# Attention with the values stationary and the turned weights moving, in a two-layer hybrid block on one Trainium2 core

## Chip, core and metric

The kernel runs on one core of a Trainium2 chip. Time is device time in microseconds (us) of one execution. The engines are PE (TensorE; its weight loads are listed as PEld), DVE (VectorE), ACT (ScalarE), POOL (GpSimd) and SP (which issues the DMAs). Each engine works through its own instructions strictly in program order and waits for others through semaphores.

## The reference, cut to what matters

Two layers run one after the other over 256 tokens of width 1024. Each layer has a token mixer with three branches (MLA attention, mLSTM, dilated attention), gates and an output projection, and then a mixture of 16 experts. The change touches the two attentions of each layer. Both have 8 heads with values of width 64 and come down to this:

```python
s = jnp.einsum('bqhd,bkhd->bhqk', qi, k).astype(jnp.float32) * scale
s = jnp.where(kpos[None, :] <= qpos[:, None], s, -jnp.inf)
p = jax.nn.softmax(s, axis=-1)
return jnp.einsum('bhqk,bkhd->bqhd', p.astype(v.dtype), v)
```

The dilated attention joins three window patterns; since there are only 256 tokens, the kernel does all three as one masked softmax, with the count of patterns that reach a key as a logarithm in the mask. What follows both branches is a product of the attention's output with a 512 x 1024 weight.

## The kernel before

All big products ("dense", lines 474 to 476) keep full precision by splitting each operand into a high part and a rest: a weight chunk is loaded by DMA into a slot, ACT copies it rounded (high part) and DVE subtracts (rest), both on line 365, and three matmuls of 128x128 by 128x512 are summed for each block. One dense product of 256 tokens by 1024 by 512 is 48 such matmuls. Between its other work DVE also multiplies the modulation weights of this and the next layer (line 284, 1024 columns each, both operands in SBUF).

Everything outside a few pinned places is ordered by the framework's scheduler: the program's text gives a stream of instructions, and the scheduler lays them out for each engine in a fixed order, in which the dense matmuls of the next projections fill the places where an attention waits. That order is fixed before the run. There is no reordering when an operand comes late.

`softmax_pv` does one attention, once for MLA and once for dilated attention in each layer, so four times. It goes through two blocks of 128 queries: t=0 with 128 keys, t=1 with 256. For each block:

- PE makes the scores of 8 heads (line 794 in MLA, line 951 in dilated attention);
- DVE adds the mask and takes the row maximum (line 731) and scales it (lines 734 and 736);
- ACT takes the exponential with its row sum (line 739), into P;
- PE turns P, 128x128 at a time (line 745), 8 times for t=0 and 16 for t=1, and ACT copies the turned weights out of PSUM into T (line 746);
- PE multiplies: T is stationary and the 64 value columns of a head move (line 750), 8 or 16 matmuls in float32, which the profile shows as two instructions each;
- DVE inverts the row sums (line 751) and multiplies the output by them while it leaves PSUM (line 752).

Then `y_transposed` turns the output (tokens on partitions) into the operand of the branch's dense product: 8 transposes on PE (line 765), two copies on ACT (line 768) and two subtractions on DVE (line 769). The mLSTM branch uses the same function with a scale.

GpSimd (POOL) has little to do: rotary embedding in MLA (lines 662 to 671), a subtraction in the router (line 1089), memsets and a few DMAs.

Of the kernel before, what the change touches and what calls it, by code (L numbers as in the profile page):

```python
# [12 lines left out]
def _warn_once_fixed(msg, *args, **kwargs):  # L13
# [6 lines left out]
F32 = mybir.dt.float32  # L20
F32R = mybir.dt.float32r
I32 = mybir.dt.int32
AF = mybir.ActivationFunctionType
OP = mybir.AluOpType
# [14 lines left out]
C_ID, C_TRI, C_TRIS, C_MLA, C_DIL, C_MLM, C_COS, C_SIN, C_IOTA = (  # L39
    0, 128, 256, 384, 640, 896, 1024, 1088, 1152)  # L40
# [31 lines left out]
def tile_block(ctx: ExitStack, tc: tile.TileContext, x_in, c_in, cst_in, sv_in, aux_in, wada_in, ws_in, out, depth=L):  # L72
    nc = tc.nc
    PE, DVE, ACT, POOL, SP = nc.tensor, nc.vector, nc.scalar, nc.gpsimd, nc.sync
# [8 lines left out]
    def fs_tile(i, dtype=F32):  # L83
        return persist.tile([128, 2048], dtype, name=f"fs{i}")

    fs = Slots([fs_tile(i) for i in range(NB)], fs_tile)

    def xs_tile(i, dtype=F32R):
        return persist.tile([128, 2048], dtype, name=f"xs{i}")
# [4 lines left out]
    xs = Slots([xs_tile(i) for i in range(4)], xs_tile, F32R)  # L94
    rs = Slots([rs_tile(i) for i in range(NR)], rs_tile, F32R)

    def mmt(name="mm"):
        return psum.tile([128, 512], F32, name=name)

    cst = persist.tile([128, N_CST], F32, name="cst")  # L100
# [79 lines left out]
    def cut(h):  # L180
        return A0 if h < 2 else 512
# [81 lines left out]
    for hf in range(2):  # L263
        hs = slice(512 * hf, 512 * hf + 512)
        p = mmt("sm")
# [76 lines left out]
    def layer(l, tail):  # L342
# [185 lines left out]
        else:  # L528
# [21 lines left out]
            for n_, (k0, k1) in enumerate(groups):  # L550
# [11 lines left out]
                p = nxt_p  # L562
# [6 lines left out]
                for j, do in enumerate((first_chunk, second_chunk, third_chunk)):  # L569
# [3 lines left out]
                    n = cut(h_)  # L573
# [68 lines left out]
        for t in range(2):  # L642
            ts = slice(128 * t, 128 * t + 128)
# [10 lines left out]
        va = v_s[:, :1024].rearrange("p (t n) -> p t n", t=2)  # L654
# [18 lines left out]
        scq = work.tile([128, 2, 8], F32, name="scq", bufs=1)  # L673
        for t in range(2):
            ts = slice(128 * t, 128 * t + 128)
# [34 lines left out]
        fs.put(cq_s, up_s, up2_s)  # L710
        pump()

        def softmax_pv(kq, masks, scale, vv, out_s):

            for t in range(2):
                nk = 128 * (t + 1)
                per = 512 // nk
                P_s, T_s = fs.get(), fs.get()
                P = P_s[:, :8 * nk].rearrange("p (h n) -> p h n", h=8)
                T = T_s[:, :8 * nk].rearrange("p (b h n) -> p b h n", b=t + 1, h=8)  # L720
                den = work.tile([128, 8], F32, name="den")
                mx = work.tile([128, 8], F32, name="mx")
                for g in range(8 // per):
                    p = mmt("sm").rearrange("p (h n) -> p h n", h=per)
                    h0 = g % 2 + 4 * (g // 2)
                    hs = slice(h0, h0 + 2 * per - 1, 2)
                    for j in range(per):
                        kq(t, h0 + 2 * j, p[:, j])
                    for j in range(per):
                        h = h0 + 2 * j  # L730
                        DVE.tensor_tensor_reduce(p[:, j], p[:, j], masks[:, 128 * (1 - t):], 1.0, -3.0e38,
                                                 OP.add, OP.max, mx[:, h:h + 1])
                    if scale is None:
                        DVE.tensor_scalar(mx[:, hs], mx[:, hs], -1.0, None, op0=OP.mult)
                    else:
                        DVE.scalar_tensor_tensor(mx[:, hs], mx[:, hs], -1.0, scale[:, t, hs], op0=OP.mult, op1=OP.mult)
                    for j in range(per):
                        h = h0 + 2 * j
                        ACT.activation(P[:, h], p[:, j], AF.Exp, scale=1.0 if scale is None else scale[:, t, h:h + 1], bias=mx[:, h:h + 1],
                                       accum_out=den[:, h:h + 1])  # L740
                for b in range(t + 1):
                    for g in range(2):
                        p = mmt("sm").rearrange("p (h n) -> p h n", h=4)
                        for j in range(4):
                            PE.transpose(p[:, j], P[:, 4 * g + j, 128 * b:128 * b + 128], ident)
                        ACT.activation(T[:, b, 4 * g:4 * g + 4], p, AF.Copy)
                po = mmt("sm").rearrange("p (h d) -> p h d", h=8)
                for h in range(8):
                    for b in range(t + 1):
                        PE.matmul(po[:, h], T[:, b, h], vv[:, b, 64 * h:64 * h + 64], start=b == 0, stop=b == t)  # L750
                DVE.reciprocal(den, den)
                DVE.tensor_tensor(out_s[:, t].rearrange("p (h d) -> p h d", h=8), po,
                                  den[:, :, None].to_broadcast([128, 8, 64]), op=OP.mult)
                fs.put(P_s, T_s)

        def y_transposed(y, scale=None):

            yt_s = xs.get(F32R)
            yt = yt_s.rearrange("p (a b n) -> p a b n", a=2, b=4)
            for bb in range(2):  # L760
                p = mmt("sm").rearrange("p (b n) -> p b n", b=2)
                for b in range(2):
                    for t in range(2):
                        c = (2 * bb + b) * 128
                        PE.transpose(p[:, b, 128 * t:128 * t + 128], y[:, t, c:c + 128], ident)
                if scale is None:
                    s = slice(2 * bb, 2 * bb + 2)
                    ACT.activation(yt[:, 0, s], p, AF.Copy)
                    DVE.tensor_tensor(yt[:, 1, s], p, yt[:, 0, s].bitcast(F32), op=OP.subtract)
                else:  # L770
                    for b in range(2):
                        s = 2 * bb + b
                        ACT.activation(yt[:, 0, s], p[:, b], AF.Copy, scale=scale(s))
                        DVE.scalar_tensor_tensor(yt[:, 1, s], p[:, b], scale(s), yt[:, 0, s].bitcast(F32),
                                                 op0=OP.mult, op1=OP.subtract)
            return yt_s, yt

        qT_s, kT_s = fs.get(), fs.get()
# [2 lines left out]
        for t in range(2):  # L781
            ts = slice(128 * t, 128 * t + 128)
            for src, dst, g in ((qc, qT, V_GQ), (kc, kT, V_GK)):
                for gg in range(2):
                    p = mmt("sm")[:96].rearrange("p (h n) -> p h n", h=4)
# [2 lines left out]
                    o = dst[:, 4 * gg:4 * gg + 4, ts]  # L788
                    ACT.activation(o, p, AF.Copy, scale=sv[:96, g:g + 1])
        fs.put(qc_s, kc_s)  # L790
        ya_s = fs.get()
        ya = ya_s[:, :1024].rearrange("p (t n) -> p t n", t=2)
        def kq_a(t, h, p):
            PE.matmul(p, qT[:, h, 128 * t:128 * t + 128], kT[:, h, :128 * (t + 1)], start=True, stop=True)

        softmax_pv(kq_a, cst[:, C_MLA:C_MLA + 256], scq, va, ya)
        fs.put(qT_s, kT_s, v_s)
        yaT_s, yaT = y_transposed(ya)
        fs.put(ya_s)
        pump()  # L800


# [105 lines left out]
        hg = work.tile([128, 4], F32, name="hg", bufs=1)  # L908
        DVE.tensor_scalar(hg, col(V_HG, 4), 0.5, None, op0=OP.mult)
        ybT_s, ybT = y_transposed(yb, lambda s: hg[:, s:s + 1])  # L910
        fs.put(mo_s)
        pump()


        dn_s, dT_s, dv_s = fs.get(), fs.get(), fs.get()
        dn = dn_s.rearrange("p (a t n) -> p a t n", a=2, t=2)
        dT = dT_s.rearrange("p (a b n) -> p a b n", a=2, b=4)
        dv = dv_s[:, :1024].rearrange("p (t n) -> p t n", t=2)
        yc = dv_s[:, 1024:].rearrange("p (t n) -> p t n", t=2)
        dq8 = work.tile([128, 1], F32, name="dq8", bufs=1)  # L920
        POOL.tensor_scalar(dq8, col(V_DQ), 0.125, None, op0=OP.mult)
        for a in range(2):
# [13 lines left out]
            for bb in range(2):  # L936
                p = mmt("sm").rearrange("p (b n) -> p b n", b=2)
# [11 lines left out]
        def kq_c(t, h, p):  # L949
            r0 = 64 * (h % 2)  # L950
            PE.matmul(p, dT[r0:r0 + 64, 0, h // 2, 128 * t:128 * t + 128], dT[r0:r0 + 64, 1, h // 2, :128 * (t + 1)],
                      start=True, stop=True)

        softmax_pv(kq_c, cst[:, C_DIL:C_DIL + 256], None, dv, yc)
        fs.put(dT_s)
        ycT_s, ycT = y_transposed(yc)
        fs.put(dv_s)
        pump()


# [2 lines left out]
        for b, (yT_s, yT) in enumerate(((yaT_s, yaT), (ybT_s, ybT), (ycT_s, ycT))):  # L963
# [10 lines left out]
            g = g_s.rearrange("p (t n) -> p t n", t=2)  # L974
# [4 lines left out]
            if b == 1:  # L979
# [6 lines left out]
                p = mmt("sm")[:, :160]  # L986
# [3 lines left out]
            for hf in range(2):  # L990
                ps = dense(yT[:, 0], yT[:, 1], 4)
                hs = slice(512 * hf, 512 * hf + 512)
# [15 lines left out]
        for kk, p in transposed(mg):  # L1008
            s = slice(2 * kk, 2 * kk + 2)
# [16 lines left out]
        def small(name, *shape):  # L1026
            return work.tile([128] + list(shape), F32, name=name, bufs=1)
# [217 lines left out]
        ex, d = small("ex", 2, 4), small("d", 2, 4)  # L1245
# [102 lines left out]
    for l in range(depth):  # L1348
        tail = layer(l, tail)
# [130 lines left out]
```

## Time and profile before

| | us |
|---|---|
| median of 3 runs (817.21 to 821.32) | 818.74 |
| the profiled execution | 815.11 |
| its span, first to last instruction | 813.3 |
| PE busy | 772.1 (95%) |
| DVE busy | 568.4 (70%) |
| ACT busy | 385.7 (47%) |
| POOL busy | 32.9 (4%) |

Busy is the share of the span in which the engine had an instruction running. Matmuls are pipelined and their ends are modelled, so how fast PE really goes is read from the distance between the starts of its instructions. Layer 0 takes the first half of the span; its MLA attention lies at 80 to 106 us and its dilated attention at 143 to 166 us. Layer 1 has them at 464 to 490 us and 541 to 565 us.

### The profile page before, as it was taken

The page shows a single profiled execution, that of the slowest core. Times are in us where ns is not written, and L with a number is a line of the kernel's source. Part 1 is how long each engine was busy: PE and PEld are TensorE (multiplying, and loading weights), DVE is VectorE, ACT ScalarE, POOL GpSimd, SP SyncE. Part 2 cuts the span into 40 slices and gives each one's busy share as a digit, 9 for nine tenths or more (in the row PEclk, how much of TensorE's full clock was granted, in tenths as well). Part 3 has the DMA queues.
Part 4 walks back from the last instruction along what each step waited for, and adds up shares of the span by engine and source line. Part 5 has one row for each costly group of instructions (what it writes and reads, how often), then busy time and mean ns, then how long its engine had stood idle before and what let it go on. Part 6 is the DMA issues. An engine that isn't in the chain of part 4 may idle for free. (4 is left out here: it accounts for less than half of the span.)

```text
span 813.3 us, 11024 instructions
## 1 busy us (share of the span) xinstructions
PE 772.1 (95%) x3772; PEld 535.4 (66%) x3772; DVE 568.4 (70%) x1422; ACT 385.7 (47%) x851; POOL 32.9 (4%) x62
## 2 busy tenths in 40 slices
PE   4999999999999979999969999999999997999996
PEld 2886888788887753333358687888888876543333
DVE  6889989978899575232488988998647576633224
ACT  5477757754355451111277674676454552411111
POOL 0103000000000000000000300000000001000000
PEclk9999999999999989999989998999999998999999
DMA  8984654889999558999847367568986636499991
GB/s 338 408 329 155 246 221 163 320 299 373 361 370 365 208 235 365 420 421 420 349 147 251 112 262 255 207 253 310 343 304 226 215 110 245 185 423 422 421 413 58
DMA packets 36109, 234.37 MB, mean 288 GB/s; under 512 B 4017, under 2 KB 4689, under 8 KB 10450
## 3 DMA queue, kind: packets, MB, share of 16 engines
q1 hardware_dynamic: 35410, 231.52, 73.5%
q0 software_dynamic: 576, 2.10, 0.7%
q8 instruction: 31, 0.51, 0.2%
q14 instruction: 28, 0.23, 0.1%
q10 hardware_dynamic: 64, 0.02, 0.0%
HBM read 232.55 MB, written 1.06 MB: 287 GB/s over the span
## 5 line engine op out<-in xcount | busy, mean ns | idle before, releaser
L365 ACT ACTIVATE rs<-wa 128x512 fp32r<-128x512 f32 (+1 forms) x224 | 135.3, 633 | 87.9 <-PE mm L475 63.3
L474 PE MATMUL mm<-rs,rs 128*128 128x512 f32 (+1 forms) x432 | 171.9, 401 | 5.0 <-ACT rs L565 4.3
L365 DVE TENSOR_TENSOR rs<-wa,rs 128x512 fp32r<-128x512 f32 (+1 forms) x224 | 148.5, 683 | 38.2 <-ACT rs L365 25.4
L475 PE MATMUL mm<-rs,rs 128*128 128x512 f32 (+1 forms) x432 | 174.3, 404 | 0.4 <-DVE rs L462 0.3
L476 PE MATMUL mm<-rs,rs 128*128 128x512 f32 (+1 forms) x432 | 173.9, 403 | 0.0
L284 DVE SCALAR_TENSOR_TENSOR wa<-wa,cb 128x1024 f32<-128x1024 f32 x90 | 108.0, 1215 | 0.1
L474 PEld LDWEIGHTS mm<-rs,rs 128*128 128x128 f32 x432 | 81.9, 191 | 21.5 <-ACT rs L565 5.5
L475 PEld LDWEIGHTS mm<-rs,rs 128*128 128x128 f32 x432 | 82.9, 192 | 16.7 <-DVE rs L566 1.1
L476 PEld LDWEIGHTS mm<-rs,rs 128*128 128x128 f32 x432 | 83.0, 192 | 15.8 <-issue 1.1
L1207 PE MATMUL mm<-wa,xs 128*64 128x512 f32 x168 | 64.4, 595 | 0.0
L1215 DVE SCALAR_TENSOR_TENSOR th<-th,mm 128x256 f32<-128x256 f32 x16 | 6.7, 421 | 81.3 <-ACT th L1214 81.3
L1207 PE MATMUL mm<-fs,xs 128*64 128x512 f32 x184 | 60.8, 595 | 0.0
L109 ACT ACTIVATE fs<-fs 128x512 fp32r<-128x512 f32 x32 | 20.2, 630 | 68.2 <-DVE fs L1238 68.2
L1214 ACT ACTIVATE th<-mm 128x256 f32<-128x256 f32 x16 | 6.1, 384 | 97.4 <-PE mm L1207 97.4
L1238 DVE TENSOR_TENSOR fs<-mm,fs 128x512 f32<-128x512 f32 x32 | 22.0, 688 | 32.8 <-PE mm L1236 32.8
L1207 PE MATMUL mm<-rs,xs 128*64 128x512 f32 x160 | 42.8, 595 | 0.0
L474 PE MATMUL mm<-rs,xs 128*128 128x512 f32 x96 | 37.6, 392 | 0.0
L476 PE MATMUL mm<-rs,xs 128*128 128x512 f32 x96 | 37.5, 391 | 0.0
L1236 PE MATMUL mm<-wa,hid 128*64 128x512 f32 x80 | 36.5, 599 | 1.1 <-ACT hid L1224 1.1
L475 PE MATMUL mm<-rs,xs 128*128 128x512 f32 x96 | 37.4, 390 | 0.0
L1207 PEld LDWEIGHTS mm<-wa,xs 128*64 128x64 f32 x168 | 19.1, 137 | 26.9 <-issue 26.6
L1236 PE MATMUL mm<-fs,hid 128*64 128x512 f32 x96 | 36.5, 598 | 0.0
(334 smaller groups left out, 1313.2 us busy)
## 6 DMA issues: line engine op xcount, KB each, us to landing
wa<-in_ws_dram SPq DMA_DIRECT2D x85, 1024.0 KB, 7.0
fs<-in_ws_dram SPq DMA_DIRECT2D x45, 1024.0 KB, 14.8
wa<-in_wada_dram SPq DMA_DIRECT2D x40, 1024.0 KB, 5.4
rs<-in_ws_dram SPq DMA_DIRECT2D x30, 1024.0 KB, 13.3
wa<-in_wada_dram SPq DMA_DIRECT2D x10, 512.0 KB, 10.0
wa<-in_ws_dram SPq DMA_DIRECT2D x6, 512.0 KB, 9.0
fs<-in_wada_dram SPq DMA_DIRECT2D x6, 512.0 KB, 10.0
fs<-row POOLq DMA_DIRECT2D x4, 512.0 KB, 7.3
```

Of the source, the lines that this page charges most:

```text
L109: return ACT.activation(h, src, AF.Copy), DVE.tensor_tensor(l, src, h.bitcast(F32), op=OP.subtract)
L284: DVE.scalar_tensor_tensor(w, w, 0.5, cb, op0=OP.mult, op1=OP.mult, accum_out=mods[l][:, 2 * i + j:2 * i + j + 1])
L365: pinned(ACT.activation(h[:, cs_], r[:, cs_], AF.Copy), DVE.tensor_tensor(lo[:, cs_], r[:, cs_], h[:, cs_].bitcast(F32), op=OP.subtract))
L474: PE.matmul(o, ah[:, kb + k, ts], hv[:, k], start=st, stop=False)
L475: PE.matmul(o, al[:, kb + k, ts], hv[:, k], start=False, stop=False)
L476: PE.matmul(o, ah[:, kb + k, ts], lv[:, k], start=False, stop=en)
L1207: queued(PE.matmul(pgu[64 * i:64 * i + 64], a, wv[i][:, k], start=kb == 0, stop=kb == 7))
L1214: ACT.activation(th, pgu[:, :256], AF.Tanh, scale=0.5)
L1215: DVE.scalar_tensor_tensor(th, th, 1.0, pgu[:, :256], op0=OP.add, op1=OP.mult)
L1236: queued(PE.matmul(py[hf][i_], hid_[:, f, i_], wv[i][:, f, hs], start=f == 0, stop=f == 1))
L1238: DVE.tensor_tensor(y, py[hf], rows[:, 1, hs], op=OP.mult)
```

## The change

The output of an attention is now made turned. The values of a head (128 keys by 64) are the stationary operand and the turned weights (128 keys by 128 queries) move; the result is 64 value columns by 128 queries. Head 2hh writes PSUM partitions 0 to 63 and head 2hh+1 partitions 64 to 127 of the same columns. So the output is already the operand of the next product, and the 8 transposes, the copies and the subtractions of `y_transposed` are gone for these two branches; a copy on ACT and a subtraction on DVE for each block of queries (lines 760 and 761) make the high part and the rest straight from PSUM.

The row sums lie on query partitions, which the turned output no longer has. So the weights are divided before they are turned: DVE inverts the sums (line 743), and POOL multiplies P by them in two halves of four heads (line 746), with 512 columns each for t=0 and 1024 for t=1. The transposes (now line 750), the copies into T (line 751) and the products (line 758) come after that. `y_transposed` stays for mLSTM.

```diff
@@ -710,8 +710,10 @@
-        def softmax_pv(kq, masks, scale, vv, out_s):
+        def softmax_pv(kq, masks, scale, vv):
+
+            yt_s = xs.get(F32R)
+            yt = yt_s.rearrange("p (a b n) -> p a b n", a=2, b=4)
             for t in range(2):
                 nk = 128 * (t + 1)
...
@@ -738,22 +740,29 @@
                         ACT.activation(P[:, h], p[:, j], AF.Exp, scale=1.0 if scale is None else scale[:, t, h:h + 1], bias=mx[:, h:h + 1],
                                        accum_out=den[:, h:h + 1])
-                for b in range(t + 1):
-                    for g in range(2):
+                DVE.reciprocal(den, den)
+                for g in range(2):
+                    hs = slice(4 * g, 4 * g + 4)
+                    POOL.tensor_tensor(P[:, hs], P[:, hs], den[:, hs, None].to_broadcast([128, 4, nk]), op=OP.mult)
+                    for b in range(t + 1):
                         p = mmt("sm").rearrange("p (h n) -> p h n", h=4)
                         for j in range(4):
                             PE.transpose(p[:, j], P[:, 4 * g + j, 128 * b:128 * b + 128], ident)
-                        ACT.activation(T[:, b, 4 * g:4 * g + 4], p, AF.Copy)
-                po = mmt("sm").rearrange("p (h d) -> p h d", h=8)
-                for h in range(8):
+                        ACT.activation(T[:, b, hs], p, AF.Copy)
+
+                po = mmt("sm").rearrange("p (h n) -> p h n", h=4)
+                for hh in range(4):
                     for b in range(t + 1):
-                        PE.matmul(po[:, h], T[:, b, h], vv[:, b, 64 * h:64 * h + 64], start=b == 0, stop=b == t)
-                DVE.reciprocal(den, den)
-                DVE.tensor_tensor(out_s[:, t].rearrange("p (h d) -> p h d", h=8), po,
-                                  den[:, :, None].to_broadcast([128, 8, 64]), op=OP.mult)
+                        for i in range(2):
+                            h = 2 * hh + i
+                            PE.matmul(po[64 * i:64 * i + 64, hh], vv[:, b, 64 * h:64 * h + 64], T[:, b, h], start=b == 0, stop=b == t)
+                ts = slice(128 * t, 128 * t + 128)
+                ACT.activation(yt[:, 0, :, ts], po, AF.Copy)
+                DVE.tensor_tensor(yt[:, 1, :, ts], po, yt[:, 0, :, ts].bitcast(F32), op=OP.subtract)
                 fs.put(P_s, T_s)
-
-        def y_transposed(y, scale=None):
+            return yt_s, yt
+
+        def y_transposed(y, scale):
...
@@ -763,16 +772,11 @@
-                if scale is None:
-                    s = slice(2 * bb, 2 * bb + 2)
-                    ACT.activation(yt[:, 0, s], p, AF.Copy)
-                    DVE.tensor_tensor(yt[:, 1, s], p, yt[:, 0, s].bitcast(F32), op=OP.subtract)
...
-        softmax_pv(kq_a, cst[:, C_MLA:C_MLA + 256], scq, va, ya)
+        yaT_s, yaT = softmax_pv(kq_a, cst[:, C_MLA:C_MLA + 256], scq, va)
         fs.put(qT_s, kT_s, v_s)
-        yaT_s, yaT = y_transposed(ya)
-        fs.put(ya_s)
...
-        softmax_pv(kq_c, cst[:, C_DIL:C_DIL + 256], None, dv, yc)
-        fs.put(dT_s)
-        ycT_s, ycT = y_transposed(yc)
-        fs.put(dv_s)
+        ycT_s, ycT = softmax_pv(kq_c, cst[:, C_DIL:C_DIL + 256], None, dv)
+        fs.put(dT_s, dv_s)
```

The scheduler lays the engines' orders out anew. On PE, the first piece below is the second block of the dilated attention in layer 0, before. Lines 474 to 476 are dense matmuls of the gates, `fs_77` is P, `rs` are split weights; "x8" counts instructions of one kind in a row.

```order
L750 MATMUL sm<-fs_74,fs_71 128x64 x8
L951 MATMUL sm<-fs_76 128x256 x8
L476 MATMUL mm<-rs_87,rs_83 128x512
L474 MATMUL mm<-rs_87,rs_83 128x512
L475 MATMUL mm<-rs_87,rs_84 128x512
L476 MATMUL mm<-rs_87,rs_83 128x512
L745 MATMUL sm<-cst,fs_77 128x128
L474 MATMUL mm<-rs_87,rs_83 128x512
L475 MATMUL mm<-rs_87,rs_84 128x512
L476 MATMUL mm<-rs_87,rs_83 128x512
L745 MATMUL sm<-cst,fs_77 128x128 x2
```

The same place in the changed kernel; at "..." stand 22 more dense matmuls.

```order
L750 MATMUL sm<-cst,fs_74 128x128 x8
L475 MATMUL mm<-rs_86,rs_84 128x512
L476 MATMUL mm<-rs_86,rs_83 128x512
L758 MATMUL sm<-fs_75,fs_76 64x128 x8
L951 MATMUL sm<-fs_77 128x256 x8
L474 MATMUL mm<-rs_86,rs_83 128x512
L475 MATMUL mm<-rs_86,rs_84 128x512
L476 MATMUL mm<-rs_86,rs_83 128x512
...
L750 MATMUL sm<-cst,fs_73 128x128 x16
L758 MATMUL sm<-fs_72,fs_76 64x128 x16
```

The transposes stood in ones and twos among the dense matmuls, four dense matmuls after the scores. Now 25 dense matmuls stand between the scores and the transposes, and then 16 transposes and 16 products follow each other without a dense matmul among them. In the eight blocks of the kernel, in order, 34, 28, 33 and 25 dense matmuls (layer 0) and 35, 27, 33 and 25 (layer 1) stand between the scores and the first transpose.

On DVE, the same block before, from the last two mask steps on. Line 284 is a modulation multiply, line 365 the rest of a weight chunk.

```order
L734 TENSOR_SCALAR mx<-mx 128x2
L284 SCALAR_TENSOR_TENSOR wa_67,mod_122<-wa_67,cb 128x1024
L731 ISA sm,mx<-sm,cst 128x256
L731 ISA mx 128x1
L284 SCALAR_TENSOR_TENSOR wa_68,mod_122<-wa_68,cb 128x1024
L734 TENSOR_SCALAR mx<-mx 128x2
L365 TENSOR_TENSOR rs_87<-wa_66,rs_87 128x512
L284 SCALAR_TENSOR_TENSOR wa_68,mod_122<-wa_68,cb 128x1024
L751 RECIPROCAL den<-den 128x8
L365 TENSOR_TENSOR rs_87<-wa_66,rs_87 128x512
```

The same place in the changed kernel:

```order
L736 TENSOR_SCALAR mx<-mx 128x2
L284 SCALAR_TENSOR_TENSOR wa_67,mod_122<-wa_67,cb 128x1024
L736 TENSOR_SCALAR mx<-mx 128x2
L284 SCALAR_TENSOR_TENSOR wa_68,mod_122<-wa_68,cb 128x1024
L365 TENSOR_TENSOR rs_86<-wa_69,rs_86 128x512
L743 RECIPROCAL den<-den 128x8
L289 TENSOR_TENSOR mod_122<-mod_122,sv_91 128x8
L284 SCALAR_TENSOR_TENSOR wa_68,mod_122<-wa_68,cb 128x1024
L365 TENSOR_TENSOR rs_86<-wa_69,rs_86 128x512
```

The reciprocal has one modulation multiply fewer ahead of it (and two rests of weight chunks fewer, which stood among the first masks, above the piece). Behind it a modulation multiply comes up at once; and now POOL's two multiplies, all 16 transposes and the products wait for that reciprocal, where only the last output multiply did.

## Rows read from the trace of the kernel before

**Rows 1.** The page, busy time of each engine, share of the span and instructions.

```profile
PE 772.1 (95%) x3772; PEld 535.4 (66%) x3772; DVE 568.4 (70%) x1422; ACT 385.7 (47%) x851; POOL 32.9 (4%) x62
```

**Rows 2.** Windows: us, each engine's busy us (instructions), granted PE clock, DMA share, GB/s.

```profile
80.00:106.00 26.00, 26.00 (x168) 22.37 (x167) 22.61 (x73) 17.56 (x51) 0.00 (x0) 1.00 0.73 274
...
500.00:507.00 7.00, 7.00 (x21) 4.59 (x18) 4.69 (x12) 3.18 (x7) 0.00 (x0) 0.51 0.65 246
```

**Rows 3.** Timeline of PE in the gates: start us, us, engine, line, operation, shapes, count.

```profile
229.62 0.39 PE L475 MATMUL mm<-rs,rs 128*128 128x512 f32 x1
...
230.07 0.39 PE L474 MATMUL mm<-rs,rs 128*128 128x512 f32 x1
```

**Rows 4.** Timeline of PE in layer 0: attention products and output transposes (two stretches).

```profile
101.03 3.46 PE L750 MATMUL sm<-fs,fs 128*128 128x64 f32 x30
...
106.05 0.82 PE L765 MATMUL sm<-cst,fs 128*128 128x128 f32 x6
```

**Rows 5.** Timeline of PE in the experts, where two 64-column products share the array.

```profile
332.71 0.59 PE L1236 MATMUL mm<-wa,hid 128*64 128x512 f32 x1
332.72 0.59 PE L1236 MATMUL mm<-fs,hid 128*64 128x512 f32 x1
333.14 0.59 PE L1236 MATMUL mm<-wa,hid 128*64 128x512 f32 x1
...
335.29 0.59 PE L1236 MATMUL mm<-fs,hid 128*64 128x512 f32 x1
335.81 0.44 PE L1222 MATMUL mm<-cst,th 128*128 128x128 f32 x2
```

**Rows 6.** Timeline of layer 0, MLA: scores of t=0 (PE), reciprocals and output multiply (DVE).

```profile
81.05 1.95 PE L794 MATMUL sm<-fs,fs 96*128 96x128 f32 x16
82.76 0.47 PE L474 MATMUL mm<-rs,rs 128*128 128x512 f32 x1
...
89.75 0.19 DVE L751 RECIPROCAL den<-den 128x8 f32<-128x8 f32 x1
...
92.48 0.69 DVE L752 TENSOR_TENSOR fs<-sm,den 128x512 f32<-128x512 f32 x1 [0.83 <-PE sm L750]
...
99.29 0.20 DVE L751 RECIPROCAL den<-den 128x8 f32<-128x8 f32 x1
```

**Rows 7.** The same in layer 0, dilated attention, with idle time and its releaser.

```profile
143.53 1.52 PE L951 MATMUL sm<-fs 64*128 64x128 f32 x16
144.99 0.51 PE L476 MATMUL mm<-rs,rs 128*128 128x512 f32 x1
...
150.81 0.19 DVE L751 RECIPROCAL den<-den 128x8 f32<-128x8 f32 x1
...
152.88 2.10 PE L951 MATMUL sm<-fs 64*128 64x256 f32 x16
154.91 0.50 PE L476 MATMUL mm<-rs,rs 128*128 128x512 f32 x1
...
157.14 0.33 PE L745 MATMUL sm<-cst,fs 128*128 128x128 f32 x1 [1.04 <-ACT fs L739]
...
161.98 0.20 DVE L751 RECIPROCAL den<-den 128x8 f32<-128x8 f32 x1
```

**Rows 8.** POOL's multiplies by shape, and a stretch of POOL and DVE in layer 0.

```profile
L1089 POOL TENSOR_TENSOR fs<-xs,fs 128x512 fp32r<-128x512 f32 x4 | 5.0, 1260 | 49.0 <-ACT xs L1088 49.0
...
64.56 1.38 POOL L668 TENSOR_TENSOR fs<-fs,fs 128x256 f32<-128x256 f32 x1 [27.87 <-DVE rs L365]
65.90 0.72 POOL L669 TENSOR_TENSOR fs<-fs,fs 128x256 f32<-128x256 f32 x1
...
64.66 0.69 DVE L365 TENSOR_TENSOR rs<-wa,rs 128x512 fp32r<-128x512 f32 x1
...
66.18 0.47 DVE L701 TENSOR_SCALAR sh<-sh 128x8 f32<-128x8 f32 x1
...
69.24 0.16 DVE L701 TENSOR_SCALAR sh<-sh 128x8 f32<-128x8 f32 x1
```

**Rows 9.** DVE's modulation multiply, timeline of layer 0.

```profile
147.24 1.22 DVE L284 SCALAR_TENSOR_TENSOR wa<-wa,cb 128x1024 f32<-128x1024 f32 x1
```

More of the change, by code (lines that the diff above doesn't have):

```diff
@@ L765, in y_transposed @@
                         PE.transpose(p[:, b, 128 * t:128 * t + 128], y[:, t, c:c + 128], ident)
-                if scale is None:
-                    s = slice(2 * bb, 2 * bb + 2)
-                    ACT.activation(yt[:, 0, s], p, AF.Copy)
-                    DVE.tensor_tensor(yt[:, 1, s], p, yt[:, 0, s].bitcast(F32), op=OP.subtract)
[L770 to L775, printed above, removed]
+                for b in range(2):
+                    s = 2 * bb + b
+                    ACT.activation(yt[:, 0, s], p[:, b], AF.Copy, scale=scale(s))
+                    DVE.scalar_tensor_tensor(yt[:, 1, s], p[:, b], scale(s), yt[:, 0, s].bitcast(F32),
+                                             op0=OP.mult, op1=OP.subtract)
             return yt_s, yt
@@ L790, in layer @@
         fs.put(qc_s, kc_s)
-        ya_s = fs.get()
-        ya = ya_s[:, :1024].rearrange("p (t n) -> p t n", t=2)
         def kq_a(t, h, p):
             PE.matmul(p, qT[:, h, 128 * t:128 * t + 128], kT[:, h, :128 * (t + 1)], start=True, stop=True)
-        softmax_pv(kq_a, cst[:, C_MLA:C_MLA + 256], scq, va, ya)
+        yaT_s, yaT = softmax_pv(kq_a, cst[:, C_MLA:C_MLA + 256], scq, va)
         fs.put(qT_s, kT_s, v_s)
-        yaT_s, yaT = y_transposed(ya)
-        fs.put(ya_s)
         pump()
```

## Prediction

> **What bounds the kernel now.** I read the page's busy times first: PE is busy for 95% of the span, DVE for 70%, POOL for 4% [rows 1]. An average says little, so I went to the windows around the attentions. From 80 to 106 us, the MLA attention of layer 0, PE is busy in all 26.00 us and DVE in 22.61 [rows 2]. The timeline says whether a busy PE is also a fast one: in the gates, two dense matmuls after another start 0.45 us apart, so 0.226 us for 512 columns [rows 3], and around the attention the same spacing holds between the transposes. So in these stages an attention costs PE time only, because dense matmuls fill every wait. There is one exception: in the second block of the dilated attention PE stood idle for 1.04 us until the first exponential was there [rows 7]; I take the same for layer 1, so 2 us in all. A gain here must come from PE's own work, and any wait that the fixed order does not cover is lost in full.
>
> **What the change takes off PE.** The 8 transposes of line 765 go, four times: 32. Six of them take 0.82 us with the last one's tail [rows 4]; the products on line 750, with the same weight load, start (3.46 - 0.27)/29 = 0.11 us apart when the last one's tail is taken off [rows 4]. At 0.11 us, 32 transposes are 3.5 us. The products: 24 matmuls of two instructions for each attention, 192 in all, at 0.11 us: 21.1 us. They become 192 instructions with 128 moving columns, of which two at a time share the array. The trace of before has nothing quite like it. From below: the experts' products with 64 columns of weights start in pairs 0.01 us apart, a pair every 0.43 us for 512 columns [rows 5]; for a quarter of the columns that is 0.11 us a pair, 96 pairs, 10.6 us. From above: the dilated scores of 128 columns need 1.46 us for 16 instructions (143.53 to 144.99, [rows 7]), 0.09 each, 17.5 us; but their order puts only some of them in pairs. The new ones alternate between the two halves as the experts' do, so I take 10.6 us: a gain of 10.5 us (3.6 at the other end). Leaving the paired form costs something: the last pair to the next transpose is 0.52 us against 0.43 [rows 5]. Entering may cost as much, so 0.2 us for each of 8 bursts, 1.6 us. PE's work falls by 3.5 + 10.5 - 1.6 = 12.4 us.
>
> DVE loses eight output multiplies of 0.69 us (one in [rows 6]), 5.5 us; copies and subtractions stay as many. As DVE is not what ends last here, I count nothing for that.
>
> **What it puts on the path.** POOL's two multiplies now stand between the reciprocal and the transposes. A multiply of 512 columns takes 1.26 us on POOL and one of 256 takes 0.72 [rows 8], so each 256 more cost 0.54 and 1024 columns 2.34 us. A block needs two: 2.5 us for t=0, 4.7 us for t=1. No such broadcast of a sum stands in the rows; 256-column multiplies with a broadcast table (line 669) are the nearest. What covers it on PE are the scores and then 34, 28, 33 and 25 dense matmuls before the first transpose, and the first half's transposes. I count from the start of a block's scores; layer 1 is taken as layer 0.
>
> - MLA, t=0. The reciprocal ends at 89.94 - 81.05 = 8.9 us [rows 6], POOL at 11.4. PE: scores 1.7, 34 x 0.226 = 7.7, four transposes 0.44: it needs the second half at 9.85. Late by 1.6 us.
> - MLA, t=1. From the output multiply's start to the reciprocal's end are 7.0 us (92.48 to 99.49, [rows 6]); now a copy on ACT comes first, 0.7: 7.7, and POOL ends at 12.4. PE: scores twice 1.7, 28 x 0.226 = 6.3, eight transposes 0.9: 10.6. Late by 1.8.
> - Dilated, t=0. Reciprocal at 151.00 - 143.53 = 7.5 [rows 7], POOL at 10.0; PE 1.46 + 7.45 + 0.44 = 9.35. Late by 0.65.
> - Dilated, t=1. The reciprocal ended 9.3 us after the scores began (152.88 to 162.18, [rows 7]). In the new order one modulation multiply (1.22 by its row, [rows 9]; 1.15 to the next start) and two weight rests (0.6 each) no longer stand ahead, but the ACT copy does: 7.5. POOL ends at 12.2. PE: 2.03 + 25 x 0.226 + 0.9 = 8.6. Late by 3.6.
>
> That is 7.65 us for each layer, 15.3 in all; less the 2 us of today, 13.3 us more idle on PE. Nothing hides it: behind the waiting transpose in PE's queue are the products and all further dense matmuls.
>
> **Whether POOL and DVE run side by side.** At 64.56 POOL's 256-column multiply took 1.38 us instead of 0.72; DVE's weight rest ran from 64.66 into that time, and POOL ended about 0.7 us after it. The next POOL multiply ran to 66.62, and a tiny DVE operation of 0.16 us that began at 66.18 took 0.47, until 66.65 [rows 8]. So these kinds of operations take turns. In the new order weight rests and modulation multiplies stand right behind each reciprocal. If DVE goes first and then in turns, POOL ends later by two rests (1.2 us) in both t=0 blocks, by one (0.6) in MLA t=1, where ACT has not made the first yet, and by a modulation multiply and a rest (1.75) in dilated t=1: 4.75 us for each layer, 9.5 in all. Bounds: 0 and 9.5. I take six tenths, 6 us, since ACT will now and then not have the next rest's input ready. DVE in turn is held for up to 8 x (1.26 + 2.34) = 28.8 us; in the MLA window it has 26.00 - 22.61 = 3.4 us free, and the waiting PE gives it the rest, so I add nothing.
>
> The Trainium skill ("SBUF — State Buffer", section "SBUF: two separate sides") says that a GpSimd operation and a DVE operation with two SBUF inputs lock the shared port pair exclusively for the whole instruction. By that rule every turn counts and the sum would be higher by the whole 9.5 us; without it, by none. The two lengthened rows agree with it.
>
> **The sum.** -12.4 + 13.3 + 6 = +6.9 us. The profiled execution took 815.11 us, its span 813.3; that execution would become 822.0. The median of the runs is 818.74, 3.6 above it, so I forecast 825.5 us. A measurement of this kernel can tell about 0.5%, 4.1 us, from no change.
>
> **The rivals.**
>
> 1. POOL is never held by DVE. Then the sum is -12.4 + 13.3 = +0.9: 819.6 us, no change to tell. For it: rests wait for ACT, which is busy with exponentials until the reciprocal. Against: [rows 8]. Chance 0.27.
> 2. The order covers POOL: the changed kernel is faster. The waits must fall below 12.4 + 2 - 4.1 = 10.3 us, against 15.3 without any turns, so POOL would need about 0.65 of the time of its rows, or the reciprocals come a good half microsecond earlier in each block. For it: before, exactly such an order left PE idle in one block of four only. With waits of 6 us the time is 810. Chance 0.18.
> 3. More than the forecast: every turn counts (+3.5), or the products do not share the array (+6.9), or PE's clock falls. The clock was granted at 0.51 from 500 to 507 us, its 1.2 GHz level, in a stretch of few matmuls: 21 in 7 us [rows 2], 2.3 us more than their 4.7 at full speed. PE idle for 5 us twice in a dilated block may bring that about again, once for each layer: +4.6. Any one of these gives 829 to 833, two of them 836. Chance 0.22.
>
> The forecast itself, slower by 4.1 to 10 us, has 0.33.
>
> **How the numbers follow.** Faster by over 0.5% is rival 2: 0.18. Within 0.5% is rival 1: 0.27. Slower is the forecast and rival 3: 0.55. The range reaches from rival 2's case to two of rival 3's: 811 to 837 us. The forecast's own range, within slower, is 823 to 829.
>
> **What would show it.** Line 746 on POOL at 1.26 and 2.34 us, or longer where a DVE operation overlaps; PE's idle time at line 750 with POOL as releaser, 13 to 25 us in the eight blocks, most of it in the two dilated t=1 blocks; line 758 starting in pairs, 0.11 us a pair; the gates no slower than before at 0.226 us. The prediction is wrong if PE shows no wait for POOL, if pairs start 0.2 us apart, or if DVE falls so far behind that dense matmuls wait for line 365 after the attention, which I have at nothing.

## The result, and the profile after

Four runs of the changed kernel gave a median of 830.04 us (826.62 to 832.44), beside 817.98 us for the kernel before: a ratio of 1.0139, 95% interval 1.009 to 1.0188. Eight later runs of the same kernel gave 823.61 us and 1.0076, interval 1.0039 to 1.0113. All twelve have a median of 826.5 us, beside the forecast of 825.5. The change makes this kernel slower by about 1%.

The two medians go with TensorE's granted clock. A run with a higher mean clock is shorter, with the changed kernel and with the kernel before alike. In 53 runs of the kernel before on the chips of the experiments, the time falls by 0.56 us for each 0.001 of mean clock. Runs at nearly the same clock compare like this:

| mean granted clock of the run | kernel before | changed kernel |
|---|---|---|
| 0.979 to 0.980 | 814.2 us (median of 6) | 822.7 us (median of 5) |
| 0.969 and below | 821.4 us (median of 18) | 830.8 us (median of 4) |
| mean clock over all runs | 0.974 (53 runs) | 0.974 (12 runs) |

So at equal clock the change costs 8 to 9.5 us. The profiled execution of the changed kernel took 832.44 us, at 0.964; that of the kernel before had 0.977. The rows below therefore hold some 6 us of lower clock that the median of the twelve runs does not (832.44 beside 826.5). They can be read for durations and waits, but not summed against the old span.

The page first: busy times, and two groups of instructions (line, engine, operation, count, busy us, mean ns, idle time before).

```profile
PE 773.7 (93%) x3740; PEld 532.8 (64%) x3740; DVE 581.3 (70%) x1414; ACT 388.4 (47%) x851; POOL 62.2 (7%) x78
...
L365 DVE TENSOR_TENSOR rs<-wa,rs 128x512 fp32r<-128x512 f32 (+1 forms) x224 | 164.5, 758 | 35.4 <-ACT rs L365 22.6
...
L746 POOL TENSOR_TENSOR fs<-fs,den 128x512 f32<-128x512 f32 (+1 forms) x16 | 31.2, 1970 | 145.8 <-PE mm L476 98.0
```

Beside [rows 1], PE fell from 95% to 93% busy, and POOL rose from 32.9 to 62.2 us: the 16 multiplies of line 746 are 31.2 us. They are also PE's largest entry in the view of waits (engine, waiting line, releaser, us in all, times, longest):

```profile
PE sm L750 <- POOL fs L746: 16.9, 16, 2.1
PE sm L546 <- ACT fs L445: 6.3, 2, 5.7
```

The second line stands in the trace of before as well. The first is new: each of the 16 multiplies is waited for. A window that was full in [rows 2] no longer is, though its clock is still 1.00 (columns as there):

```profile
80.00:106.00 26.00, 24.51 (x135) 20.05 (x134) 25.19 (x76) 17.74 (x50) 3.60 (x3) 1.00 0.76 283
```

The timeline of the first block of layer 0's MLA attention (start us, us, engine, line; idle time before it and its releaser):

```profile
91.56 0.19 DVE L743 RECIPROCAL den<-den 128x8 f32<-128x8 f32 x1
...
91.67 4.13 DVE L365 TENSOR_TENSOR rs<-wa,rs 128x512 fp32r<-128x512 f32 x4
...
91.88 2.77 POOL L746 TENSOR_TENSOR fs<-fs,den 128x512 f32<-128x512 f32 x2 [16.37 <-PE mm L476]
...
93.26 0.66 PE L750 MATMUL sm<-cst,fs 128*128 128x128 f32 x4 [0.70 <-POOL fs L746]
...
94.71 0.66 PE L750 MATMUL sm<-cst,fs 128*128 128x128 f32 x4 [0.79 <-POOL fs L746]
...
95.52 1.19 PE L758 MATMUL sm<-fs,fs 128*64 128x128 f32 x16
...
96.64 1.13 PE L796 MATMUL sm<-fs,fs 96*128 96x256 f32 x4
```

PE waits twice, for either half of the heads. Four transposes at 0.11 us from 93.26 would have let the next begin at 93.70; it began 1.0 us later, of which 0.79 shows as idle. The 16 products, which at 0.11 us each [rows 4] would be 1.8 us, now take 96.64 - 95.52 = 1.12. DVE's four weight rests take 4.13 us, where four with nothing in their way take 2.5 (experiment 4). The second block of the dilated attention shows why:

```profile
175.83 1.21 DVE L284 SCALAR_TENSOR_TENSOR wa<-wa,cb 128x1024 f32<-128x1024 f32 x1
...
176.01 5.09 POOL L746 TENSOR_TENSOR fs<-fs,den 128x1024 f32<-128x1024 f32 x2 [9.92 <-PE mm L476]
...
176.97 2.37 DVE L365 TENSOR_TENSOR rs<-wa,rs 128x512 fp32r<-128x512 f32 x1
178.85 1.09 PE L750 MATMUL sm<-cst,fs 128*128 128x128 f32 x8 [2.08 <-POOL fs L746]
179.27 1.85 DVE L292 SCALAR_TENSOR_TENSOR mod<-mod,sv 128x8 f32<-128x8 f32 x1
...
181.15 0.69 PE L750 MATMUL sm<-cst,fs 128*128 128x128 f32 x2 [1.21 <-POOL fs L746]
```

DVE's modulation multiply began first and kept its usual 1.21 us [rows 9]. POOL's first multiply could work only after it. The weight rest that came next took 2.37 us, to 179.34: some 0.5 us beyond the transposes that POOL's first multiply released at 178.85. An operation of 8 columns (line 292, two inputs, at most 0.19 us in the kernel before) then took 1.85 us beside POOL's second. They take turns, as in [rows 8].

### The profile page after: what moved, and what is told of

Read it like the earlier page. It is cut to its first block, busy times and chain, and to the rows that moved or that the text cites. A ratio compares the mean times of both kernels' runs of the same rounds, so it can differ in the third digit from the quotient of the medians.

```text
span 830.5 us, 11014 instructions
## 1 busy us (share of the span) xinstructions
PE 773.7 (93%) x3740; PEld 532.8 (64%) x3740; DVE 581.3 (70%) x1414; ACT 388.4 (47%) x851; POOL 62.2 (7%) x78
## 5 line engine op out<-in xcount | busy, mean ns | idle before, releaser
L365 DVE TENSOR_TENSOR rs<-wa,rs 128x512 fp32r<-128x512 f32 (+1 forms) x224 | 164.5, 758 | 35.4 <-ACT rs L365 22.6
L475 PEld LDWEIGHTS mm<-rs,rs 128*128 128x128 f32 x432 | 83.1, 192 | 17.2 <-DVE rs L566 1.1
L746 POOL TENSOR_TENSOR fs<-fs,den 128x512 f32<-128x512 f32 (+1 forms) x16 | 31.2, 1970 | 145.8 <-PE mm L476 98.0
```

Of the source, the lines that this page charges most:

```text
L365: pinned(ACT.activation(h[:, cs_], r[:, cs_], AF.Copy), DVE.tensor_tensor(lo[:, cs_], r[:, cs_], h[:, cs_].bitcast(F32), op=OP.subtract))
L475: PE.matmul(o, al[:, kb + k, ts], hv[:, k], start=False, stop=False)
L746: POOL.tensor_tensor(P[:, hs], P[:, hs], den[:, hs, None].to_broadcast([128, 4, nk]), op=OP.mult)
```

## The experiments

**1. Division cut to 8 columns.** One line of the changed kernel. Most of the division is left out, so that the waits go and the order nearly stays:

```
-POOL.tensor_tensor(P[:, hs], P[:, hs], den[:, hs, None].to_broadcast([128, 4, nk]), op=OP.mult)
+POOL.tensor_tensor(P[:, hs, :8], P[:, hs, :8], den[:, hs, None].to_broadcast([128, 4, 8]), op=OP.mult)
```

> Leaves out most of the division: GpSimd multiplies only 8 columns of each head, so every instruction and nearly the whole order of TensorE stay (32, 24, 29, 24 dense matmuls ahead of the transposes in layer 0). Theory (TensorE's work fell by 14 us, and all the loss is waiting for GpSimd plus the clock falls that this waiting brings): the waits at the transposes fall from 19.5 us to under 3, the clock falls between 80 and 600 us go from five to about one, and the time is about 14 us under the kernel before, 803 to 806 us. Rival 1 (the clock falls come from the new products, not from the waits): waits gone, clock falls stay, 809 to 812. Rival 2 (the new products save nothing): 816 or more.

Measured: 806.04 us, ratio 0.9838 (0.9803 to 0.9873). The expectations, here and below, give the changed kernel's waits as 19.5 us. The view's idle time for them is 16.9, and the waits measured here are read from that view. One line is left of this kind:

```profile
PE sm L750 <- POOL fs L746: 5.3, 7, 2.2
```

The theory stands in the main: without the bulk of GpSimd's work the new form is 12 us faster than before, of which some 8 us remain at equal clock (at 0.980 to 0.982 the kernel before took 813 to 815 us). Rival 2 is out. The waits fell by 11.6 us, not by 14 or more, since the transposes still wait for an instruction of POOL. The mean clock of its six runs was 0.981, so rival 1, that the products bring the clock down, is out too.

**2. No pairs.** All products of one half of the rows ahead of those of the other:

```
-for hh in range(4):
-    for b in range(t + 1):
-        for i in range(2):
+for i in range(2):
+    for hh in range(4):
+        for b in range(t + 1):
```

> The changed kernel with the two heads of a pair no longer one behind the other: all products of the upper half of the rows, then all of the lower half. Theory (the saving comes from two products that share the array): starts 0.11 us apart instead of a pair every 0.11, 96 x 0.11 = 10.6 us more, 839 to 842 us. Rival (an instruction of 128 columns takes 0.055 us in any order, so pairs are not the cause): same as the changed kernel, 828 to 832.

Measured: 830.81 us, ratio 1.0163 (1.0111 to 1.0214): by its time the theory's range was missed and the rival's met. But the mean clock of its four runs was 0.974, that of the changed kernel's first four 0.969. Beside all twelve runs of the changed kernel (826.5 us at 0.974) it is some 4 to 5 us slower at equal clock, under half of the theory's 10.6. Its rows show the products lengthened: the 32 instructions of the second MLA block in layer 0, first here and then in the changed kernel:

```profile
109.02 3.33 PE L758 MATMUL sm<-fs,fs 128*64 128x128 f32 x32
```

```profile
110.43 1.97 PE L758 MATMUL sm<-fs,fs 128*64 128x128 f32 x32
```

Its waits for POOL are 16.7 us, so they do not explain the missing part. The question was put again where no waits blur it:

**3. No pairs, with the division on DVE** (edit 2 on the kernel of experiment 4):

> The kernel with the division on DVE, whose transposes wait for nothing, with the products of a block in the order upper half, then lower half. Theory (two neighbouring products in different halves share the array, and without waits and clock falls the saving shows in the time): the four products' blocks of a layer pair become about 0.5 and 1.4 us longer each, 7 to 8 us in all, so 807 to 810 us beside 800.8 for the kernel with pairs. Rival (the pairs save nothing that is on the path): 799 to 802 us.

Measured: 813.23 us, ratio 0.994 (0.9912 to 0.9968), 12.4 us above the kernel of experiment 4. Its mean clock was also lower, 0.976 beside 0.982; at 0.978 its runs took 811 to 813 us, against 800 to 802 at 0.979 to 0.981. At equal clock some 8 to 10 us are the pairs', so the theory's 7 to 8 are about right, though its range of times was missed. Its timeline, the second block of the dilated attention:

```profile
181.71 3.33 PE L758 MATMUL sm<-fs,fs 128*64 128x128 f32 x32
184.96 0.50 PE L476 MATMUL mm<-rs,xs 128*128 128x512 f32 x1
```

and the same 32 instructions in pairs, in the kernel of experiment 4:

```profile
177.44 1.97 PE L758 MATMUL sm<-fs,fs 128*64 128x128 f32 x32
179.33 0.50 PE L475 MATMUL mm<-rs,xs 128*128 128x512 f32 x1
```

3.25 us against 1.89: 0.10 and 0.06 for an instruction. The pairs are the gain. Why experiment 2 shows only a part of it in its time stays open.

**4. The division on DVE.**

```
-POOL.tensor_tensor(P[:, hs], P[:, hs], den[:, hs, None].to_broadcast([128, 4, nk]), op=OP.mult)
+DVE.tensor_tensor(P[:, hs], P[:, hs], den[:, hs, None].to_broadcast([128, 4, nk]), op=OP.mult)
```

> The same multiplies on DVE instead of GpSimd. Theory (GpSimd's time behind the reciprocal is what costs): a multiply takes about 0.6 us for 512 and 1.2 us for 1024 columns, the waits at the transposes fall under 5 us, the weight rests are no longer held (their sum falls from 164 to about 149 us), the time is 803 to 809 us. Rival (DVE, busy for 70% of the span, cannot take 15 us more where it has only some us free, and dense matmuls wait for line 365 instead): 815 to 822 us.

Measured: 800.81 us, ratio 0.9782 (0.9747 to 0.9817), 17 us faster than the kernel before and under the theory's range. At equal clock it is some 12 us: at 0.982, this kernel's mean, the kernel before took 813.2. In the view of waits no transpose waits for a division any more. The second block of the MLA attention, and the weight rests on the page:

```profile
103.58 0.21 DVE L743 RECIPROCAL den<-den 128x8 f32<-128x8 f32 x1
...
103.70 0.65 DVE L365 TENSOR_TENSOR rs<-wa,rs 128x512 fp32r<-128x512 f32 x1
...
104.25 2.36 DVE L746 TENSOR_TENSOR fs<-fs,den 128x1024 f32<-128x1024 f32 x2
...
105.64 0.40 PE L474 MATMUL mm<-rs,rs 128*128 128x512 f32 x1
105.88 1.04 PE L750 MATMUL sm<-cst,fs 128*128 128x128 f32 x8
...
106.52 2.50 DVE L365 TENSOR_TENSOR rs<-wa,rs 128x512 fp32r<-128x512 f32 x4
```

```profile
L365 DVE TENSOR_TENSOR rs<-wa,rs 128x512 fp32r<-128x512 f32 (+1 forms) x224 | 147.3, 685 | 23.4 <-PE mm L475 12.1
```

Reciprocal to the end of the division: 3.0 us with a weight rest in between, and PE starts its transposes right behind a dense matmul. The rests are back at 685 ns. DVE took over the multiplies (eight at 0.7 us, eight at 1.2, some 15 us in all) and did not become the bound.

**5. The old products, with the division on GpSimd.** The kernel before, with the multiplies ahead of the transposes and the output multiply made a copy:

```
+DVE.reciprocal(den, den)
+for g in range(2):
+    hs = slice(4 * g, 4 * g + 4)
+    POOL.tensor_tensor(P[:, hs], P[:, hs], den[:, hs, None].to_broadcast([128, 4, nk]), op=OP.mult)
...
-DVE.reciprocal(den, den)
-DVE.tensor_tensor(out_s[:, t].rearrange("p (h d) -> p h d", h=8), po,
-                  den[:, :, None].to_broadcast([128, 8, 64]), op=OP.mult)
+DVE.tensor_copy(out_s[:, t].rearrange("p (h d) -> p h d", h=8), po)
```

> Only the division of the change: the kernel before, with the weights divided on GpSimd ahead of their transposes, products and turned outputs as before, and DVE's output multiply made a copy. Theory (the division costs 17 us of waits by itself): 834 to 838 us, waits at the transposes of 17 to 20 us. Rival (the waits come with the shorter products, since less of TensorE's work lies beside GpSimd): waits under 12 us, 824 to 830 us.

Measured: 836.6 us at a clock of 0.974, 843.5 at 0.967, 848.4 at 0.959 and 856.0 at 0.947; the first three give a ratio of 1.0309 (1.0238 to 1.0381). The kernel before took 816.4 to 816.6 in its four runs at 0.975 to 0.976, and 821.4 at 0.967 to 0.969. The division on GpSimd alone costs 20 to 22 us at equal clock, a little above the theory's 17. Its waits have the theory's size (line 748 is the transposes here, 744 the multiply):

```profile
PE sm L748 <- POOL fs L744: 17.0, 16, 1.9
```

**6. The old products, with the division on DVE** (the same with DVE in POOL's place):

> The same with the multiplies on DVE: the division ahead of the transposes without GpSimd. Theory (TensorE's work is that of the kernel before, and the division lies beside dense matmuls): 815 to 819 us, so that values stationary are worth 14 to 17 us of the kernel with the division on DVE. Rival (the gain of that kernel came from where DVE divides, not from the products): 800 to 806 us.

Measured: 813.24 us, ratio 0.9946 (0.992 to 0.9973), clock 0.981. At 0.979 to 0.980 the kernel before took 814.2: the division ahead of the transposes is free if DVE does it. The step to experiment 4 is 12.4 us at nearly the same clock (0.981 and 0.982; by the 0.56 us above, that difference is some 0.8 us of it). That is what values stationary, in pairs and without output transposes, are worth, and less than the 14 to 17 us expected here.

**7. Scores of both blocks ahead.** In the changed kernel, the loop over t is cut in two, scores to multiplies first, transposes and products after:

```
+                blocks.append((t, nk, P_s, P))
+            for t, nk, P_s, P in blocks:
+                T_s = fs.get()
```

> The changed kernel with the scores, exponentials and GpSimd multiplies of both blocks ahead of the transposes of the first. Theory (a wait is what the order does not cover): GpSimd's work for the first block lies beside the second block's scores, the waits fall from 19.5 us to about 10, the time is 815 to 821 us. Rival (the fixed order only moves the dense matmuls, so that the chain of both blocks is waited for in one piece): waits of 18 us or more, 828 to 833 us.

Measured: 814.53 us, ratio 0.9962 (0.9932 to 0.9992), just under the theory's range; the waits about as the theory had them, 8.7 us:

```profile
PE sm L756 <- POOL fs L746: 8.7, 11, 1.4
```

Cover, not only GpSimd's speed, decides. At equal clock this kernel matches the one before (its mean clock was 0.978), so the remaining waits still eat the gain.

**8. A reciprocal for each half.**

```
-DVE.reciprocal(den, den)
 for g in range(2):
     hs = slice(4 * g, 4 * g + 4)
+    DVE.reciprocal(den[:, hs], den[:, hs])
```

> The changed kernel with one reciprocal for each half of the heads, so that GpSimd can begin the first half of a t=1 block while the exponentials of the second half still run. The order answers with fewer dense matmuls ahead of the first transposes (29, 19, 33, 21 in layer 0). Theory (GpSimd's two multiplies in a row behind the last exponential are what is waited for): the waits of the t=1 blocks fall from 11.3 us to about 5, all waits from 19.5 to 12 to 14 us, the time is 819 to 825 us. Rival (the order takes back what GpSimd gains): waits of 18 us or more, 828 to 832 us.

Measured: 829.11 us, ratio 1.0137 (1.0087 to 1.0186): the rival. Its waits, and the second MLA block of layer 0:

```profile
PE sm L750 <- POOL fs L746: 18.1, 14, 2.1
```

```profile
94.92 3.29 PE L796 MATMUL sm<-fs,fs 96*128 96x256 f32 x14
...
100.78 2.72 POOL L746 TENSOR_TENSOR fs<-fs,den 128x1024 f32<-128x1024 f32 x1 [8.30 <-DVE den L745]
...
103.55 1.09 PE L750 MATMUL sm<-cst,fs 128*128 128x128 f32 x8 [1.01 <-POOL fs L746]
...
104.51 0.17 DVE L745 RECIPROCAL den<-den 128x4 f32<-128x4 f32 x1
...
104.84 2.69 POOL L746 TENSOR_TENSOR fs<-fs,den 128x1024 f32<-128x1024 f32 x1 [1.35 <-DVE den L745]
...
107.59 1.09 PE L750 MATMUL sm<-cst,fs 128*128 128x128 f32 x8 [1.55 <-POOL fs L746]
```

GpSimd does begin early, 5.9 us after the start of the scores (14 of the 16 stand in the run at 94.92) instead of 8.5 (96.64 to 105.16 in the changed kernel). But the fixed order put only 19 dense matmuls ahead of the first transposes instead of 28, and the second reciprocal ended 9.8 us after the scores began in any case.

**9. Weight rests with one input.** Line 365's subtraction becomes a multiply by zero of the high half, with an accumulator as a second output, so the low halves of the mixer's weights are left out:

```
-DVE.tensor_tensor(lo[:, cs_], r[:, cs_], h[:, cs_].bitcast(F32), op=OP.subtract)
+DVE.tensor_scalar(lo, h, 0.0, 0.0, op0=OP.mult, op1=OP.add, accum_out=a)
```

> The changed kernel with line 365's subtraction (two inputs in SBUF) replaced on DVE by a multiply by zero with one input, for the weights of the mixer; it leaves the low halves of those weights out. Modulation multiplies, which read two inputs, stay. Theory (DVE operations with two inputs and GpSimd's multiplies take turns): a block's two multiplies take 2.1 us (t=0) and 3.8 us (t=1) where no modulation multiply lies beside them, instead of 2.5 to 3.4 and 4.2 to 5.1, line 365's operations are not lengthened, and the waits fall from 19.5 to 12 to 15 us: 819 to 825 us. Rival (GpSimd is slow by itself, and the lengthened rows are chance): the pairs keep their times, waits of 18 us or more, 826 to 831 us.

Measured: 838.40 us, ratio 1.0261 (1.022 to 1.0303): no theory had it that slow. Its rows settle the turns nevertheless (line 751 is the multiply here, 755 the transposes, 355 the rest):

```profile
107.04 3.75 POOL L751 TENSOR_TENSOR fs<-fs,den 128x1024 f32<-128x1024 f32 x2 [11.72 <-DVE den L748]
...
107.18 0.69 DVE L355 TENSOR_SCALAR_CACHE_REDUCE rs<-rs 128x512 fp32r<-128x512 f32 x1 [0.29 <-ACT rs L370]
...
109.01 2.86 DVE L284 SCALAR_TENSOR_TENSOR wa<-wa,cb 128x1024 f32<-128x1024 f32 x1
...
571.63 2.04 POOL L751 TENSOR_TENSOR fs<-fs,den 128x512 f32<-128x512 f32 x2 [64.90 <-PE mm L481]
```

```profile
PE sm L755 <- POOL fs L751: 16.7, 15, 2.6
...
PE sm L946 <- DVE fs L938: 4.4, 4, 2.6
```

One-input rests beside a multiply take 0.69 us, and the pair takes 3.75 or 2.04 us, in four blocks of eight. In the other four a modulation multiply, with two inputs, began ahead of POOL, and the pairs take 2.84 to 2.86 and 4.56. The modulation multiply that came up later, at 109.01, takes 2.86 beside the same POOL instruction. So the turns are between operations with two inputs and POOL's multiply, and this form of a one-input operation is free of them. The accumulators gave DVE 264 more small instructions, and PE now waits for DVE elsewhere (4.4 us at line 946). The order moved too: 28, 29 and 29 dense matmuls cover three of the t=0 blocks, where 33, 35 and 33 stood, and 29, 33 and 28 cover three of the t=1 blocks, where 25, 27 and 25 stood. The waits for GpSimd stayed at 16.7 us, so the theory's fall to 12 to 15 was missed. Of the 12 us by which this kernel is above the changed one, some 4 go with its clock of 0.969. The rest is traced only in part, and its time tells nothing of the turns.

**10. The changed kernel again.**

> The changed kernel, unaltered, in more runs, for its interval and its clock. If the clock falls belong to the change, its runs have a lower mean clock than those of the kernel before on the same chip (0.975 there so far) and the time is 827 to 831 us. If the low clock of its profiled execution (0.964) was chance, the mean clocks are alike and the time is 825 to 827 us, some 10 us over the kernel before at the same clock.

Measured: 823.61 us, as told above, with a mean clock of 0.977, and under both expected ranges. The kernel before had 0.975 on that chip. The low clock of the first runs was chance, as far as 53 and 12 runs can tell. The waits were 17.2 us, beside 16.9.

## Why the prediction was right, by its steps

| step | forecast | shown |
|---|---|---|
| PE's own work | -12.4 us | -12.4 us, at equal clock some -11.6 (experiment 4 against 6) |
| waits for POOL and its turns with DVE | +13.3 +6 = +19.3 us | +20 to +22 us at equal clock (experiment 5 against before) |
| sum | +6.9 us | +8 to +9.5 us at equal clock |

**PE's work.** Products in pairs 0.11 us apart, from [rows 5], held; the 0.2 us for a burst were about right (16 instructions in 1.12 us, where 8 pairs at 0.11 are 0.88). That -12.4 stands on both sides is luck in its last digits: the pairs' part, forecast at 10.5 us, was measured as 8 to 10.

**The waits.** All eight blocks wait, as predicted. The view of waits gives 16.9 us, and each of the 16 costs about 0.2 us more until the next transpose, 20 us; less 2 us of before, 18. The two dilated t=1 blocks are not as far ahead of the others as forecast: 2.08 + 1.21 us of idle time in layer 0, where 3.6 and up to 1.75 were counted.

**GpSimd's price** was too high and the turns too low, and the errors cancel in part. Without turns a pair takes 2.04 us (t=0) or 3.75 (t=1), not 2.5 and 4.7 (experiment 9): the nearest rows, with two full inputs, overstate a multiply by a broadcast column. Eight blocks are then 4 x (2.04 + 3.75) = 23.2 us; line 746 was busy for 31.2, so 8.0 us are turns, where I took 6 out of 0 to 9.5. The price was 5.6 us too high (28.8 forecast), the turns 2 us too low.

The rule of the Trainium skill ("SBUF — State Buffer", section "SBUF: two separate sides") that the pair of ports is locked for a whole instruction agrees with the 2.37 us of a rest behind a running multiply. The same page of the Trainium skill (section "Who interferes with whom") says that a DVE operation with at most one SBUF input, outside the two-port modes, does not contend. That agrees with the 0.69 us of experiment 9. One of the two lengthened rows to which the prediction points is not a case of two inputs: line 701 in [rows 8] has one. Its 0.47 us instead of 0.16 shows that not every one-input operation is free, and what sets it apart from the rest of experiment 9 was not tested.

**DVE behind.** I added nothing for DVE being held. The rests grew from 148.5 us on the page of before to 164.5 (mean 683 and 758 ns), and no wait of PE for line 365 joined the largest. The rows' sum, -12.4 + 18, is 2 to 4 us under the time at equal clock; no row was found for that remainder, and the held rests may be part of it.

**The rivals.** By its first four runs (830.04 us) the kernel lay in rival 3's range, 829 to 833; all twelve, whose mean clock is that of the kernel before, put it into the forecast's own 823 to 829. Rival 1 fell with the turns. Rival 2 (the order covers GpSimd) is not this kernel; experiment 7 shows how far an order can go. Of rival 3, 8.0 of the 9.5 us of turns count. The products do share the array, and the mean clock is no lower: the falls in the profiled execution, three of them in t=1 blocks (at 180, 504 and 583 us), looked like a cause until the twelve runs had the same mean clock as the 53 of before. The windows around the first of the three, where PE had been idle for 2.1 us (columns as in [rows 2]; 0.50 is the level of 1.2 GHz):

```profile
174.00:180.00 6.00, 3.86 (x21) 2.81 (x19) 6.00 (x10) 3.54 (x11) 3.99 (x2) 0.99 0.69 247
180.00:186.60 6.60, 5.45 (x40) 4.85 (x40) 4.85 (x8) 1.83 (x4) 1.10 (x1) 0.50 0.84 320
```

## What to carry to other kernels

A form that saves TensorE work can still lose if it moves an operation from behind the products to ahead of them: price the new link of the chain on the engine that will run it, with what that engine shares. Here the same change with the division on DVE is 2.2% faster than the kernel before (1.5% at equal clock), and with it on GpSimd 1% slower. When a fixed order is computed from costs, making a link faster need not shorten the wait, since the order moves its cover as well.

## What was not expected of the hardware

DVE multiplies 512 columns by a broadcast column in 0.7 us and 1024 in 1.2 us, GpSimd in 1.02 and 1.9 us with nothing in its way. The executions of the kernel before spread over 813 to 823 us with a mean clock of 0.982 to 0.967: a whole per cent, as much as the effect sought. The kernels with few waits for GpSimd had the higher clocks here (0.981 and 0.982 in experiments 1, 4 and 6), but experiment 3, with none, had 0.976, and the kernel before, with hardly any, 0.974; what sets it stays open.
